# SwiGLU gate and up with the weights stationary: one product for all tokens, PSUM pools by stage, two banks by turns for the turned tokens

## The chip, the cores and the metric

The kernel runs on one core of one Trainium2 chip. The metric is device time in microseconds for one execution: the median of three runs, 1009.31 us, with 1009.22 as the lowest and 1009.62 as the highest. The profile is of one more execution of the same program.

The core has five engines with instruction queues of their own. TensorE (PE) multiplies matrices, VectorE (DVE), ScalarE (ACT) and GpSimd (POOL) work on vectors, and SyncE (SP) issues the DMA transfers. Each works through its own queue in order, and an instruction that needs another engine's result waits on a semaphore. PE writes to PSUM, which has eight banks of 512 fp32 columns; DVE and ACT read results from there.

## What is computed

Two layers, each a feed-forward block, a mixer and a second feed-forward block, for 256 tokens of width 1024 in fp32:

```python
def swiglu(x, w_in, w_out):
    gate, up = jnp.split(x @ w_in, 2, axis=-1)
    return (jax.nn.silu(gate) * up) @ w_out

for layer in range(DEPTH):                      # 2
    x = x + 0.5 * swiglu(rms_norm(x, norm_ffn1[layer]), w_ffn1_in[layer], w_ffn1_out[layer])
    h = rms_norm(x, norm_mix[layer])
    x = x + (conv_nsa_mixer(h, ...) if layer % 2 == 0 else stick_breaking_mixer(h, ...))
    x = x + 0.5 * swiglu(rms_norm(x, norm_ffn2[layer]), w_ffn2_in[layer], w_ffn2_out[layer])
return rms_norm(x, norm_final)
```

The inner width of a feed-forward block (FFN here) is 2816. The stages in time are FFN1, mixer 0, FFN2, FFN3, mixer 1, FFN4.

## The kernel before

**Precision.** PE multiplies in fp32r. Each operand is split into a high part and a low rest, and a product in fp32 quality is three products: high by high, high by low, low by high (`mm3`). A weight arrives by DMA in a tile `raw`; ACT copies it to `wh` in fp32r, DVE subtracts to get `wl` (`split`, lines 84 and 85). Both come in tiles of 128 x 1024. The activations get `XH` by an ACT copy that multiplies by the norm's gain (line 156) and `XL` by DVE (line 157).

**Turning.** Products need the width of x on the partitions. So x (128 tokens x 1024, two token tiles) is turned by PE's transposes, four 128 x 128 pieces into one PSUM bank (`turn_pe`, line 143), and each piece is evacuated by ACT (XH) and then by DVE (XL). The factor of the RMS norm is one number per token: ACT sums squares (line 126, `scr`), POOL adds (line 130, `ms`) and raises to -0.5 (line 131, `rs`). In front of a mixer x is multiplied by rs first (line 192, `xs`) and then turned. In front of an FFN x itself is turned and rs is applied later.

**FFN.** 11 chunks of 256 inner columns. For a chunk and a token tile, gate and up together are one PSUM bank of 512 columns (`gu`): the stationary operand is the 128 x 128 piece of XH or XL, the moving one 512 columns of weights. Eight pieces of the width by three products give 24 products of 512 columns per token tile and chunk, 528 in all (`gu_mm`). `act` applies rs with silu (line 226) and the product with up (line 228) per token. h then has tokens on the partitions and is turned for the second matrix (`act_turn`: PE's transposes, line 235, in pairs; ACT's `hh`, DVE's `hl`). The output products (`out_mm`, 264 of 512 columns) collect in four banks `po`; the last ones of each quarter are followed by the update of x (line 300).

**Order.** A scheduler sets the order of each engine's queue from the program; `flush` runs the turns that stand in `pending` at a place that the program names. At the start of an FFN that follows another stage the first chunk takes token tile 0 whole, calls `flush` after its fourth piece (so tile 1 is turned then), and goes on to tile 1. At the kernel's start loads, splits and evacuations of the first chunk are written in an order by hand. The three PSUM pools, `ps_gu` with 2 banks, `ps_tr` with 2 and `ps_po` with 4, are open throughout.

**Mixers.** Each begins with products of V (280 columns in mixer 0, 512 in mixer 1) and goes on to products of 256 columns (`project_T`, lines 353 to 355), each with a weight piece as the stationary operand. `OutProj` ends them, with the update of x in line 327.

Of the kernel before, what the change touches and what calls it, by code (L numbers as in the profile page):

```python
# [21 lines left out]
NCH = 11  # L22
# [24 lines left out]
def trunk_kernel(ctx: ExitStack, tc: tile.TileContext, a: dict):  # L47
# [13 lines left out]
    ps_gu = ctx.enter_context(tc.tile_pool(name="ps_gu", bufs=2, space=PSUM))  # L61
    ps_tr = ctx.enter_context(tc.tile_pool(name="ps_tr", bufs=2, space=PSUM))
    ps_po = ctx.enter_context(tc.tile_pool(name="ps_po", bufs=4, space=PSUM))

    def bank(pool, tag):
        return pool.tile([P, 512], F32, tag=tag, name=tag)

# [26 lines left out]
    nc.sync.dma_start(gains, a["gains"])  # L94
# [5 lines left out]
    gfin = [None]  # L100
    XH = [None]
    XL = [None]
    RS = [None]

    def new_xt():
        XH[0] = acts.tile([P, ND, T], F32R, tag="XH", name="XH")
        XL[0] = acts.tile([P, ND, T], F32R, tag="XL", name="XL")
# [3 lines left out]
    half = const.tile([P, 1], F32, name="half")  # L111
    G.memset(half, -0.5)
# [15 lines left out]
    def rms(t):  # L128
        ms = small.tile([P, 1], F32, tag="ms", name="ms")
        G.tensor_scalar(ms, sq[t][:, 0:1], sq[t][:, 1:2], EPS, op0=ALU.add, op1=ALU.add)  # L130
        latest["pool"] = G.tensor_tensor(RS[0][:, t:t + 1], ms, half, op=ALU.pow)
# [8 lines left out]
    def turn_pe(src):  # L140
        pt = bank(ps_tr, "tr")
        for k in range(4):
            PE.transpose(pt[:, k * P:(k + 1) * P], src[:, k * P:(k + 1) * P], ident)  # L143
        return pt

    def turn(t, hf, src, ni):

        pt = turn_pe(src)
        evacuate(pt, t, hf, ni, range(4))

    def evacuate(pt, t, hf, ni, ks):
        for k in ks:
            dt = hf * 4 + k
            g = gains[:, ni, dt:dt + 1]
            ts = slice(t * P, (t + 1) * P)
            latest["act"] = S.activation(XH[0][:, dt, ts], pt[:, k * P:(k + 1) * P], AF.Copy, scale=g)  # L156
            latest["dve"] = V.scalar_tensor_tensor(XL[0][:, dt, ts], pt[:, k * P:(k + 1) * P], g, f(XH[0][:, dt, ts]),  # L157
                                                   op0=ALU.mult, op1=ALU.subtract)
# [3 lines left out]
    def flush():  # L162
        for go in pending:
            go()
        pending.clear()

    def updated(t, hf, then):
# [5 lines left out]
        if kind == "ffn":  # L173
            pending.append(lambda: turn(t, hf, halves(t, hf), ni))
            if hf:
                rms(t)
            return
# [11 lines left out]
        if kind == "mix":  # L189
            for h in range(2):  # L190
                hs = slice(h * 512, (h + 1) * 512)
                V.tensor_scalar(o[:, hs], halves(t, h), r, None, op0=ALU.mult)
                pending.append(lambda h=h, hs=hs: turn(t, h, o[:, hs], ni))
# [18 lines left out]
    def ffn(w_in, w_out, then, first=None):  # L212
        xh, xl, rs = XH[0], XL[0], RS[0]
        po = {}
        hT = {}
# [6 lines left out]
        hs = {}  # L222

        def act(t, pg):
            sg = small.tile([P, T], F32, tag="sg", name="sg", bufs=2)
            latest["silu"] = S.activation(sg, pg[:, :T], AF.Silu, scale=rs[:, t:t + 1])  # L226
            h = small.tile([P, T], F32, tag="h", name="h", bufs=2)
            V.scalar_tensor_tensor(h, pg[:, T:], rs[:, t:t + 1], sg, op0=ALU.mult, op1=ALU.mult)  # L228
            hs[t] = h

        def act_turn(c, t):
            h = hs[t]
            pt = bank(ps_tr, "tr")
            for k in range(2):
                PE.transpose(pt[:, k * P:(k + 1) * P], h[:, k * P:(k + 1) * P], ident)  # L235
            hh = small.tile([P, 2, P], F32R, tag="hh", name="hh", bufs=6)
            hl = small.tile([P, 2, P], F32R, tag="hl", name="hl", bufs=6)
            pv = pt[:, :T].rearrange("p (k q) -> p k q", k=2)
            S.activation(hh, pv, AF.Copy)
            V.tensor_tensor(hl, pv, f(hh), op=ALU.subtract)  # L240
            hT[c, t] = hh, hl

        def out_mm(c, t, k, wo, hfs=(0, 1)):
            hh, hl = hT[c, t]
            wh, wl = wo[k]
            for hf in hfs:
# [3 lines left out]
                mm3(po[t, hf], hh[:, k], hl[:, k], wh[:, cs], wl[:, cs], c == 0 and k == 0, c == NCH - 1 and k == 1)  # L250

        wos = {}
        for c in range(NCH):
            if first and c == 0:
                w = first
            else:
                w = units(w_in[c, 0]) + units(w_in[c, 1])
            pg = [bank(ps_po, "po") if c == 1 else bank(ps_gu, "gu") for _ in range(NT)]
            if (c == 0 and not first) or c == NCH - 1:
                for t in range(NT):  # L260
                    for dt in range(ND):
                        gu_mm(pg[t], t, dt, w)
                        if c == 0 and t == 0 and dt == 3:
                            flush()
                        if c and t and dt == 2:
                            act_turn(c, 0)
                    act(t, pg[t])
# [703 lines left out]
```

## Time and profile before

| | |
|---|---|
| median of 3 runs | 1009.31 us (1009.22 to 1009.62) |
| the profiled execution | 1010.14 us |
| its span, first to last instruction | 1008.4 us |
| PE busy | 992.9 us, 98% |
| DVE busy | 598.7 us, 59% |
| ACT busy | 542.2 us, 54% |
| mean granted clock of PE | 0.999 of 2.4 GHz |

Times below are microseconds from the start of the span. Starts tell more than durations on PE: products are pipelined, one of 512 columns has a duration of 0.39 us, and the next starts 0.23 behind it. A bracket at the end of a timeline row is the idle time of the engine ahead of that row, and what ended it. In a row of the timeline equal instructions that follow each other are one row with their number behind an x.

### The profile page before, as it was taken

Reading aid. Unit: us, or ns where it says so; the run is one execution under the profiler, and the core shown is the slowest. Engines: PE = TensorE matmul, PEld = TensorE weight load, DVE = VectorE, ACT = ScalarE, POOL = GpSimd, SP = SyncE. Lnnn points to the kernel's source line nnn. Section 1 sums busy time; section 2 is a strip of 40 time slices with the busy share of each in tenths; the row PEclk is TensorE's granted clock in tenths of the full one; section 3 lists DMA queues with packets and bytes.
Section 4 is the critical chain, followed back from the end, with each engine's and each line's share of the span. In section 5 each row is a group of like instructions: output and inputs, shape, how many; then the busy total and the mean of one; then the engine's idle time right before and its main releaser. Section 6 shows DMA issues by size and latency. Waiting matters only on the chain.

```text
span 1008.4 us, 13048 instructions
## 1 busy us (share of the span) xinstructions
PE 992.9 (98%) x5048; PEld 825.3 (82%) x5048; DVE 598.7 (59%) x891; ACT 542.2 (54%) x944; POOL 51.5 (5%) x97
## 2 busy tenths in 40 slices
PE   8999999999999999999999999999999999999997
PEld 6888888788888888888878888887898788888885
DVE  5655555599855655555575555546777575555553
ACT  7544444587545544444474444445887474444443
POOL 4000000132111000000000000000000010000001
PEclk9999999999999999999999999999999999999999
DMA  8745454454433654545445454553632255554521
GB/s 319 271 170 205 170 206 135 146 194 161 164 126 110 228 205 169 206 170 204 168 168 201 175 200 175 198 177 125 247 118 98 84 205 210 172 204 172 204 105 42
DMA packets 26702, 176.72 MB, mean 175 GB/s; under 512 B 3344, under 2 KB 3472, under 8 KB 5904
## 3 DMA queue, kind: packets, MB, share of 16 engines
q1 hardware_dynamic: 26640, 175.89, 49.1%
q8 instruction: 39, 0.64, 0.3%
q14 instruction: 23, 0.19, 0.1%
HBM read 174.83 MB, written 1.05 MB: 174 GB/s over the span
## 4 chain that ended last, share of the span: by engine, by line
PE 74%; issue 18%; DVE 3%; ACT 2%; POOL 1%; DMA 1%; SPq 0%; POOLq 0%; ACTq 0%
PE gu L203 11%; PE gu L202 11%; PE gu L204 11%; PE po L202 8%; PE po L203 8%; PE po L204 8%; PE gu L353 3%; PE gu L355 3%; PE gu L354 3%; PE tr L235 1%; PE tr L143 1%; ACT wh L84 1%; DVE wl L85 1%; DMA raw<-in_w_in 1%; PE po L787 1%
## 5 line engine op out<-in xcount | busy, mean ns | idle before, releaser
L85 DVE TENSOR_TENSOR wl<-raw,wh 128x1024 fp32r<-128x1024 f32 (+3 forms) x388 | 397.2, 1038 | 295.1 <-ACT wh L84 293.8
L84 ACT ACTIVATE wh<-raw 128x1024 fp32r<-128x1024 f32 (+3 forms) x396 | 349.3, 899 | 317.0 <-PE gu L204 169.3
L202 PE MATMUL gu<-wh,XH 128*128 128x512 f32 (+1 forms) x688 | 267.6, 389 | 1.4 <-ACT XH L156 1.3
L204 PE MATMUL gu<-wh,XL 128*128 128x512 f32 (+1 forms) x688 | 266.9, 388 | 0.1
L203 PE MATMUL gu<-wl,XH 128*128 128x512 f32 (+1 forms) x688 | 266.6, 387 | 0.0
L202 PEld LDWEIGHTS gu<-wh,XH 128*128 128x128 f32 x688 | 129.1, 188 | 29.7 <-ACT XH L156 3.8
L204 PEld LDWEIGHTS gu<-wh,XL 128*128 128x128 f32 x688 | 129.1, 188 | 26.8 <-DVE XL L157 0.6
L203 PEld LDWEIGHTS gu<-wl,XH 128*128 128x128 f32 x688 | 129.2, 188 | 26.6 <-DVE wl L85 0.4
L202 PE MATMUL po<-wh,hh 128*128 128x512 f32 x352 | 143.9, 409 | 0.0
L204 PE MATMUL po<-wh,hl 128*128 128x512 f32 x352 | 138.0, 392 | 0.0
L203 PE MATMUL po<-wl,hh 128*128 128x512 f32 x352 | 137.8, 392 | 0.0
L353 PE MATMUL gu<-XH,wh 128*128 128x256 f32 x288 | 83.7, 291 | 1.6 <-DVE u L476 1.2
L355 PE MATMUL gu<-XH,wl 128*128 128x256 f32 x288 | 81.4, 283 | 0.0
L354 PE MATMUL gu<-XL,wh 128*128 128x256 f32 x288 | 81.4, 283 | 0.0
L204 PEld LDWEIGHTS po<-wh,hl 128*128 128x128 f32 x352 | 66.1, 188 | 14.1
L203 PEld LDWEIGHTS po<-wl,hh 128*128 128x128 f32 x352 | 66.4, 189 | 11.5
L202 PEld LDWEIGHTS po<-wh,hh 128*128 128x128 f32 x352 | 66.2, 188 | 11.3
L226 ACT ACTIVATE sg<-gu,rs 128x256 f32<-128x256 f32 x80 | 38.0, 475 | 61.3 <-PE gu L204 61.2
L353 PEld LDWEIGHTS gu<-XH,wh 128*128 128x128 f32 x288 | 55.1, 191 | 2.0 <-issue 1.3
L228 DVE SCALAR_TENSOR_TENSOR h<-gu,rs,sg 128x256 f32<-128x256 f32 x80 | 38.7, 483 | 30.2 <-ACT sg L226 30.2
L354 PEld LDWEIGHTS gu<-XL,wh 128*128 128x128 f32 x288 | 55.1, 191 | 0.1
L355 PEld LDWEIGHTS gu<-XH,wl 128*128 128x128 f32 x288 | 55.0, 191 | 0.0
(207 smaller groups left out, 874.5 us busy)
## 6 DMA issues: line engine op xcount, KB each, us to landing
raw<-in_w_in SPq DMA_DIRECT2D x86, 1024.0 KB, 4.7
raw<-in_w_out SPq DMA_DIRECT2D x44, 1024.0 KB, 4.7
raw<-in_w_ab SPq DMA_DIRECT2D x10, 1024.0 KB, 4.8
raw<-in_w_qk SPq DMA_DIRECT2D x8, 1024.0 KB, 4.8
raw<-in_w_out_ab SPq DMA_DIRECT2D x4, 1024.0 KB, 4.7
raw<-in_w_v SPq DMA_DIRECT2D x4, 1024.0 KB, 4.7
raw<-in_w_out_sb SPq DMA_DIRECT2D x4, 1024.0 KB, 4.9
raw<-in_w_in SPq DMA_DIRECT2D x8, 256.0 KB, 6.3
```

The costliest lines, as they stand in the source:

```text
L84: S.activation(h[:, ms], r[:, ms], AF.Copy)
L85: eng.tensor_tensor(l[:, ms], r[:, ms], f(h[:, ms]), op=ALU.subtract)
L143: PE.transpose(pt[:, k * P:(k + 1) * P], src[:, k * P:(k + 1) * P], ident)
L202: PE.matmul(out, lh, rh, start=first, stop=False)
L203: PE.matmul(out, lh, rl, start=False, stop=False)
L204: PE.matmul(out, ll, rh, start=False, stop=last)
L226: latest["silu"] = S.activation(sg, pg[:, :T], AF.Silu, scale=rs[:, t:t + 1])
L228: V.scalar_tensor_tensor(h, pg[:, T:], rs[:, t:t + 1], sg, op0=ALU.mult, op1=ALU.mult)
L235: PE.transpose(pt[:, k * P:(k + 1) * P], h[:, k * P:(k + 1) * P], ident)
L353: PE.matmul(pq, wh[:, dt], XH[0][:, dt], start=dt == 0, stop=False)
L354: PE.matmul(pq, wh[:, dt], XL[0][:, dt], start=False, stop=False)
L355: PE.matmul(pq, wl[:, dt], XH[0][:, dt], start=False, stop=dt == ND - 1)
```

## The change

Gate and up get their operands the other way round. The weights of w_in are laid out in 22 chunks of 128 inner columns. The stationary operand is a 128 x 128 piece of weights; the moving one is the tokens: `XX` holds XH and XL side by side, so wh meets all 512 columns of `XX` in one product (line 263), and wl meets the 256 columns of XH in another (line 265). The products stand in runs: for half of the width eight of 512 columns (four pieces, gate and up), then eight of 256. The result, in a pair of banks (gate and up; XL's half to be added to XH's half), has the inner columns on the partitions, so the transposes of h go away.

The factor rs now lies along the columns. `factor` spreads it over all partitions: ident times rs on DVE, one fp32 product with a matrix of ones on PE, a copy on ACT to `RB`. `act` then takes, per chunk: ACT copies the XL half out of PSUM, DVE adds the XH half, DVE multiplies by RB, ACT silu, DVE the product with up, ACT hh, DVE hl.

The PSUM pools other than `ps_po` are opened per stage (`stage`): in an FFN two pairs of banks, in a mixer two banks `gu` and two `tr`. They are closed at its end. `turn` puts pieces into two banks by turns; at the end of an FFN these two are the two halves of a gu pair (one tile), in a mixer two tiles `tr`, at the start of an FFN two banks of `po`. The first products of an FFN need all tokens. At the kernel's start both token tiles of a half are turned into the same banks and evacuated together, and the loads are reordered; chunk 0 and chunk 1 take their first halves, then their second ones. Between two FFNs the last output products go by halves of the width, (0,0), (1,0), (0,1), (1,1). The output products of chunk c-2 stand behind gu of chunk c.

The core of the diff:

```diff
-        def gu_mm(pg, t, dt, w):
-            (wh, wl), o = w[dt // 2], (dt % 2) * 512
-            ts = slice(t * P, (t + 1) * P)
-            mm3(pg, xh[:, dt, ts], xl[:, dt, ts], wh[:, o:o + 512], wl[:, o:o + 512], dt == 0, dt == ND - 1)
+        def gu_mm(c, w, i):
+            if c not in pgs:
+                pgs[c] = pair()
+            pg = pgs[c]
+            for wp in range(2):
+                for k in range(4):
+                    dt = 4 * i + k
+                    for s in range(2):
+                        lh = w[i][wp][:, (2 * k + s) * P:(2 * k + s + 1) * P]
+                        if wp == 0:
+                            PE.matmul(pg[:, s], lh, xx[:, dt].rearrange("p a q -> p (a q)"), start=dt == 0, stop=False)
+                        else:
+                            PE.matmul(pg[:, s, :T], lh, xx[:, dt, 0], start=False, stop=dt == ND - 1)
...
+        def factor():
+            dg = small.tile([P, 2, T], F32, tag="gus", name="dg", bufs=1)[:, 0]
+            for t in range(NT):
+                V.tensor_scalar(dg[:, t * P:(t + 1) * P], ident, rs[:, t:t + 1], None, op0=ALU.mult)
+            pr = bank(ps_po, "po")[:, :T]
+            PE.matmul(pr, ones, dg, start=True, stop=True)
+            S.activation(RB, pr, AF.Copy)
...
+                S.activation(gu[:, :, ts], pg[:, :, tl], AF.Copy)
+                V.tensor_tensor(gu[:, :, ts], pg[:, :, ts], gu[:, :, ts], op=ALU.add)
+                V.tensor_tensor(gu[:, :, ts], gu[:, :, ts], RB[:, None, ts].to_broadcast([P, 2, T // n]), op=ALU.mult)
+                latest["silu"] = S.activation(sg[:, ts], gu[:, 0, ts], AF.Silu)
+                V.tensor_tensor(sg[:, ts], gu[:, 1, ts], sg[:, ts], op=ALU.mult)
+                S.activation(hh[:, ts], sg[:, ts], AF.Copy)
+                V.tensor_tensor(hl[:, ts], sg[:, ts], f(hh[:, ts]), op=ALU.subtract)
...
+    def stage(mixer):
+        es = ExitStack()
+        for k in ("gu", "tr") if mixer else ("gu",):
+            st[k] = es.enter_context(tc.tile_pool(name="ps_" + k, bufs=2, space=PSUM))
+        return es
+    def pair(name="gu"):
+        return st["gu"].tile([P, 2, 512], F32, tag="gu", name=name)
...
+    def turn(t, dts, src, ni, get):
+        ts = slice(t * P, (t + 1) * P)
+        banks = get()
+        pt = {dt: banks[n % 2][:, n // 2 * P:(n // 2 + 1) * P] for n, dt in enumerate(dts)}
+        for dt in dts:
+            PE.transpose(pt[dt], src[:, dt * P:(dt + 1) * P], ident)
+        for dt in dts:
+            evacuate((XH[0][:, dt, ts], XL[0][:, dt, ts]), pt[dt], dt, ni)
...
+        order = [(0, 0), (1, 0), (0, 1), (1, 1)] if then[0] == "ffn" else [(0, 0), (0, 1), (1, 0), (1, 1)]
+        def banks():
+            both_ = pair()
+            return both_[:, 0], both_[:, 1]
```

The order of the built programs at three places. First PE at the kernel's start, behind the warm-up products. Line 143 before and line 932 now are transposes of x, lines 202 to 204 before and 263 and 265 now gate and up, line 244 the factor product. Before:

```order
L143 MATMUL tr<-ident,x 128x128 x8
L202 MATMUL gu<-wh,XH 128x512
L203 MATMUL gu<-wl,XH 128x512
L204 MATMUL gu<-wh,XL 128x512
...
L203 MATMUL gu<-wl,XH 128x512
L143 MATMUL tr<-ident,x 128x128 x8
L204 MATMUL gu<-wh,XL 128x512
```

Now:

```order
L932 MATMUL po<-ident,x 128x128 x16
L263 MATMUL gu<-XX,wh 128x512 x8
L265 MATMUL gu<-XX,wl 128x256 x8
...
L244 MATMUL po<-dg,ones 128x256
L263 MATMUL gu<-XX,wh 128x512 x8
```

Before, 20 products of gu stand between the two groups of eight transposes; now all sixteen stand ahead of the first, and the factor product stands behind four runs of sixteen.

Second DVE at the end of FFN1 and the entry into mixer 0. Lines 300 before and 338 now update x, 192 and 210 make xs, 157 and 162 evacuate a turned piece as the low part, 85 and 96 split weights. Before:

```order
L300 SCALAR_TENSOR_TENSOR x<-po,x 128x512
L157 SCALAR_TENSOR_TENSOR XL<-tr,gains,XH 128x128 x2
L85 TENSOR_TENSOR wl<-raw,wh 128x560
L157 SCALAR_TENSOR_TENSOR XL<-tr,gains,XH 128x128
L192 TENSOR_SCALAR xs<-x,rs 128x512 x2
L157 SCALAR_TENSOR_TENSOR XL<-tr,gains,XH 128x128 x8
```

Now:

```order
L338 SCALAR_TENSOR_TENSOR x<-po,x 128x512
L162 SCALAR_TENSOR_TENSOR XX<-gu,gains,XX 128x128
L210 TENSOR_SCALAR xs<-x,rs 128x512
L162 SCALAR_TENSOR_TENSOR XX<-gu,gains,XX 128x128
L210 TENSOR_SCALAR xs<-x,rs 128x512
L162 SCALAR_TENSOR_TENSOR XX<-gu,gains,XX 128x128 x4
L162 SCALAR_TENSOR_TENSOR XX<-tr,gains,XX 128x128 x8
```

Before, three pieces of tile 0 stand behind the last update of x, and their bank is not one that V's products write; now six pieces out of the gu pair stand there, one between the two xs and four behind them, and V's first product on PE waits for the last of them.

Third DVE where FFN3 follows FFN2, from the last update of x; line 242 makes dg. Before:

```order
L300 SCALAR_TENSOR_TENSOR x<-po,x 128x512
L85 TENSOR_TENSOR wl<-raw,wh 128x1024
L157 SCALAR_TENSOR_TENSOR XL<-tr,gains,XH 128x128 x2
L85 TENSOR_TENSOR wl<-raw,wh 128x1024
L157 SCALAR_TENSOR_TENSOR XL<-tr,gains,XH 128x128 x2
```

Now:

```order
L338 SCALAR_TENSOR_TENSOR x<-po,x 128x512
L96 TENSOR_TENSOR wl<-raw,wh 128x1024
L162 SCALAR_TENSOR_TENSOR XX<-gu,gains,XX 128x128
L242 TENSOR_SCALAR dg<-ident,rs 128x128
L96 TENSOR_TENSOR wl<-raw,wh 128x1024
L162 SCALAR_TENSOR_TENSOR XX<-gu,gains,XX 128x128
L162 SCALAR_TENSOR_TENSOR XX<-po,gains,XX 128x128 x2
L162 SCALAR_TENSOR_TENSOR XX<-gu,gains,XX 128x128
L162 SCALAR_TENSOR_TENSOR XX<-po,gains,XX 128x128 x2
L162 SCALAR_TENSOR_TENSOR XX<-gu,gains,XX 128x128
```

The splits stood among the evacuations before, too; but then the first gu products of tile 0 needed none of these. Now the first gu product waits for the last XX out of the gu pair in this list.

## Rows read from the trace of the kernel before

**Rows 1.** The page: busy time of each engine, share of the span, instructions.
```profile
PE 992.9 (98%) x5048; PEld 825.3 (82%) x5048; DVE 598.7 (59%) x891; ACT 542.2 (54%) x944; POOL 51.5 (5%) x97
```

**Rows 2.** Timeline of PE in FFN1 (start us, duration us, engine, line, operation).
```profile
65.49 0.39 PE L202 MATMUL po<-wh,hh 128*128 128x512 f32 x1
...
71.43 0.39 PE L202 MATMUL gu<-wh,XH 128*128 128x512 f32 x1
...
82.31 0.39 PE L202 MATMUL po<-wh,hh 128*128 128x512 f32 x1
```

**Rows 3.** Timeline of PE at the entry into the first mixer.
```profile
196.29 0.29 PE L202 MATMUL gu<-wh,XH 128*128 128x280 f32 x1
...
199.26 0.29 PE L204 MATMUL gu<-wh,XL 128*128 128x280 f32 x1
...
206.21 0.28 PE L353 MATMUL gu<-XH,wh 128*128 128x256 f32 x1
...
209.91 0.28 PE L354 MATMUL gu<-XL,wh 128*128 128x256 f32 x1
```

**Rows 4.** A window on FFN2: busy us of each engine, granted clock, DMA share, GB/s.
```profile
319.60:507.00 187.40, 187.40 (x853) 153.91 (x852) 106.41 (x130) 93.43 (x136) 2.56 (x4) 1.00 0.54 191
```

**Rows 5.** Timeline of PE at an fp32 product of 256 columns.
```profile
255.20 0.70 PE L675 MATMUL po<-pcT,VC 128*128 128x256 f32 x2
...
255.86 0.28 PE L354 MATMUL gu<-XL,wh 128*128 128x256 f32 x1
```

**Rows 6.** Group of one line (busy us, mean ns | idle before): copy of 512 from PSUM.
```profile
L794 ACT ACTIVATE e<-po 128x512 f32<-128x512 f32 x8 | 4.8, 599 | 2.0 <-PE po L789 1.9
```

**Rows 7.** Timeline of DVE where FFN3 follows FFN2.
```profile
508.26 0.68 DVE L300 SCALAR_TENSOR_TENSOR x<-po,x 128x512 f32<-128x512 f32 x1
508.86 1.22 DVE L85 TENSOR_TENSOR wl<-raw,wh 128x1024 fp32r<-128x1024 f32 x1
510.00 0.60 DVE L157 SCALAR_TENSOR_TENSOR XL<-tr,gains,XH 128x128 fp32r<-128x128 f32 x2
510.52 1.22 DVE L85 TENSOR_TENSOR wl<-raw,wh 128x1024 fp32r<-128x1024 f32 x1
```

**Rows 8.** The tile x in the first 14 us: how long its loads take to land.
```profile
DMA to landing us min/median/max: 3.4/5.5/6.8
```

**Rows 9.** Timeline of SyncE's DMA queue at the start: the last two loads of x.
```profile
4.06 0.91 SPq L859 DMA_DIRECT2D x<-in_x  x2
```

**Rows 10.** Timeline of PE at the start of the kernel.
```profile
1.24 4.02 PE L877 MATMUL gu<-warm 128*128 128x512 bf16 x9 [1.24 <-DVE warm L110]
...
9.69 0.76 PE L202 MATMUL gu<-wh,XH 128*128 128x512 f32 x2 [0.98 <-ACT XH L156]
...
13.84 0.48 PE L204 MATMUL gu<-wh,XL 128*128 128x512 f32 x1
```

**Rows 11.** Timeline of DVE at the entry into the first mixer.
```profile
196.57 0.68 DVE L300 SCALAR_TENSOR_TENSOR x<-po,x 128x512 f32<-128x512 f32 x1
...
199.24 1.82 DVE L192 TENSOR_SCALAR xs<-x,rs 128x512 f32<-128x512 f32 x2 [0.42 <-POOL rs L131]
...
202.20 0.61 DVE L157 SCALAR_TENSOR_TENSOR XL<-tr,gains,XH 128x128 fp32r<-128x128 f32 x2 [0.51 <-ACT XH L156]
202.99 0.61 DVE L157 SCALAR_TENSOR_TENSOR XL<-tr,gains,XH 128x128 fp32r<-128x128 f32 x2 [0.17 <-ACT XH L156]
```

**Rows 12.** Timeline of PE where FFN3 follows FFN2.
```profile
507.03 0.39 PE L202 MATMUL gu<-wh,XH 128*128 128x512 f32 x1
...
517.11 0.39 PE L202 MATMUL gu<-wh,XH 128*128 128x512 f32 x1
```

**Rows 13.** Timeline of PE at the entry into the second mixer.
```profile
695.85 0.39 PE L202 MATMUL gu<-wh,XH 128*128 128x512 f32 x1
...
718.99 0.28 PE L353 MATMUL gu<-XH,wh 128*128 128x256 f32 x1
```

**Rows 14.** Group of one line: the weight loads of the 256-column products.
```profile
L353 PEld LDWEIGHTS gu<-XH,wh 128*128 128x128 f32 x288 | 55.1, 191 | 2.0 <-issue 1.3
```

More of the change, by code (lines that the diff above doesn't have):

```diff
@@ L231, in act_turn @@
[L231 to L241, printed above, removed]
@@ new lines, in weights @@
+        def weights(c):
+            if first and c < 2:
+                return first[c]
+            return units(w_in[c])
+        def gu_mm(c, w, i):
[11 more added lines that the diff above has]
+                            PE.matmul(pg[:, s, :T], lh, xx[:, dt, 0], start=False, stop=dt == ND - 1)
@@ new lines, in out_mm @@
+                mm3(po[t, hf], hh[:, ts], hl[:, ts], wh[:, cs], wl[:, cs], c == 0, c == NF - 1)
+        es = stage(False)
+        w = [weights(0), weights(1)]
+        gu_mm(0, w[0], 0)
+        flush(lambda: two("po"))
+        gu_mm(1, w[1], 0)
+        gu_mm(0, w[0], 1)
+        factor()
+        act(0)
+        gu_mm(1, w[1], 1)
+        act(1)
+        for c in range(2, NF):
+            w = weights(c)
+            for i in range(2):
+                gu_mm(c, w, i)
+            act(c, NT if c == NF - 1 else 1)
+            if c % 2 == 0 and c < NF - 2:
+                wos[c // 2 - 1] = units(w_out[c // 2 - 1])
+            if c < NF - 2:
+                for t in range(NT):
+                    out_mm(c - 2, t)
@@ new lines, in ffn @@
+        if then == ("mix", 2):
+            switch("exp_and_others", latest["silu"])
+        for i in range(NF // 2 - 2, NF // 2):
+            wos[i] = units(w_out[i])
+        if then[0] != "end":
+            new_xt()
+        new_rs()
+        order = [(0, 0), (1, 0), (0, 1), (1, 1)] if then[0] == "ffn" else [(0, 0), (0, 1), (1, 0), (1, 1)]
+        def banks():
+            both_ = pair()
+            return both_[:, 0], both_[:, 1]
+        for t, hf in order[:2]:
+            for c in range(NF - 4, NF - 1):
+                out_mm(c, t, (hf,))
@@ L306, in trunk_kernel @@
+        for n, (t, hf) in enumerate(order):
+            for c in range(NF - 1 if n < 2 else NF - 4, NF):
+                out_mm(c, t, (hf,))
+                if c == NF - 3 and then[0] == "ffn":
+                    flush(banks)
+            V.scalar_tensor_tensor(halves(t, hf), po[t, hf], 0.5, halves(t, hf), op0=ALU.mult, op1=ALU.add)
+            if n == 2 and then[0] != "ffn":
+                flush(banks)
+            updated(t, hf, then)
+        es.close()
     class OutProj:
@@ L343, in rest @@
                     self.mm(1, n, (hf,))
+                    if hf and n == 4:
+                        flush(lambda: two("tr"))
                 if hf == 0:
-                    flush()
+                    flush(lambda: two("tr"))
                 self.done(1, hf)
@@ L751, in mixer1 @@
                     if dt == 4:
[L752 removed]
+                        flush(lambda: two("tr"))
                 S.activation(V1[:, t, hf * 512:(hf + 1) * 512], pv, AF.Copy)
[L754 to L755 removed]
+        _, YH, YL = parts("YY1")
         NQ = 2
```

228 lines of the change are left out of this document (87 added, 141 removed).

## The prediction

> **What bounds the kernel now.** I read the page first. TensorE (PE) is busy 992.9 of 1008.4 us [rows 1], so time changes only where PE does other work or stands. Then PE's timeline, for what a product costs: 48 products of 512 columns start within 10.88 us (71.43 to 82.31), 0.2267 each [rows 2]; 31 products of 256 columns, each with weights of its own, within 3.70 us, 0.120 each; 23 of 280 columns within 2.97, 0.129 each [rows 3]. From 65.49 to 71.43, 5.94 us, stand 24 output products and two pairs of transposes of h [rows 2]; 24 x 0.2267 is 5.44, so a pair costs 0.25. In FFN2 PE is busy in 187.40 of 187.40 us at a granted clock of 1.00 [rows 4]: what the vector engines do there is hidden. So the steady part can gain only by less work on PE, and the edges between stages, where PE now hardly stands, have much to lose. Those I read last.
>
> **The change, steady part.** Gate and up keep their columns: 528 products of 512 become 352 of 512 and 352 of 256. At the rates above that is 119.7 against 122.0 us per FFN, 2.3 more (every product carries a fixed piece, and there are 176 more). The 44 transposes, 22 pairs, go: 5.5 less. New is the factor product in fp32. An fp32 product of 256 columns runs before as two passes; it and one product behind it take 0.66 us [rows 5], so it costs 0.54. A run of eight 512s is followed by one of 256s, 44 times; that 512s and 256s of two kinds follow each other I price at 0 to 12 ns a change, the 13 ns being what a product takes beyond its columns (0.2267 against 512 columns at 2.4 GHz, 0.2133), so 0 to 0.5 us. Per FFN 5.5 - 2.3 - 0.54 - 0.25 = 2.4 less (2.1 to 2.7), **9.6 us less for four**.
> The new vector work does not reach PE there. For one chunk of 128 columns DVE has three weight splits of 1024 (1.14 each), the add and the multiplication (0.68 each, as the x update [rows 7]) and two shorter ones: at most 6.1 us, where PE needs 5.55 + 12 x 0.2267 = 8.27. ACT has less, its copy of 512 from PSUM at 0.60 [rows 6]. Two pairs of banks leave each pair a whole chunk's time to be read. I put nothing.
> The Trainium skill, "TensorE: Matmul & The Clock Gate", "Back-to-back issue gap", gives N/2.4 + 2.5 ns between starts, 109 and 216 ns here; by it 176 more products would cost 0.4 us a FFN in place of 2.3, the gain would be 17 us and the sum below 7 us lower. The rows show 120 and 227, and the measurement decides.
>
> **The change, edges.** With weights stationary one product takes all 256 tokens, so the first product of a FFN waits for XH and XL of both token tiles. Before, tile 0 began while tile 1 was still turned. And PSUM pools are closed by stage: the first product into the new pool waits for the last reader of the tile that lay there.
>
> (a) Start. All 16 transposes of x stand ahead of the first gu on PE. The last quarter of x is issued at about 4.54 us and landings took up to 6.8, so 11.3 [rows 8, 9]; the same 1.75 MB lie ahead of it after the change. With four transposes gu starts at 11.8, and with 20 products PE is at 16.3. Before, those 20 and all transposes are done at 13.84 [rows 10]. **+2.5.**
> (b) The first act. In FFN1 the factor product comes behind gu of chunk 1, and the third pair of banks is the first again: it waits for the copy of the factor (0.38 by a copy of 512 at 0.60 [rows 6] less half its columns), the copy of gus (0.60) and the add (0.68), with hops 1.9. In FFN2 to 4 half a chunk of products (2.8 us) stands between, which covers it. **+1.9.**
> (c) Into the first mixer. The turned xs of token tile 0 lies in a gu pair, both banks in one tile, and the first V product goes into its bank. So it waits for the eighth XX<-gu on DVE, and ahead of the last five of these DVE has the x update of the last half and both xs of tile 1. From the start of that update to that of xs 2.67 us pass, the two xs take 1.82 (POOL splits weights beside them), and XH and XL of one piece by turns 0.79 [rows 11]. The update begins 0.2 behind the last output product; one XL stands between the two xs, four pairs follow, the first with its ACT copy under xs: 0.2 + 2.67 + 0.26 + 1.82 + 0.35 + 3 x 0.79 = 7.7. I take 7.3, since XL overlaps its neighbours. Then 24 x 0.129 for tile 0, 0.87 for eight transposes, 0.5 until their first copy, 24 x 0.129 and 0.2 of small waits (two tr tiles let ACT and DVE work side by side): 15.1 us from the last output product to the first product of 256 columns. Before 9.92, from 196.29 to 206.21 [rows 3]. **+5.2.**
> (d) Into FFN2, and likewise FFN4. Behind the last output product DVE still has two splits of 1024, the x update and six XL before the first gu may go. The next start on DVE comes 1.14 behind a split, 0.60 behind an x update, 0.26 behind an XL [rows 7]: 2 x 1.14 + 0.60 + 5 x 0.26 + 0.35 + 0.24 for one ACT copy = 4.75; eight transposes (0.87) lie inside, so PE stands 3.9. Before, gu of tile 0 ran over it [rows 4], 0.2 was lost. **+3.7 each, +7.4.**
> (e) FFN2 into FFN3. gu waits for the last reader of the pair with x's turned tile. DVE: rest of a split 0.3, two XL 0.5, x update 0.6, a wait for ACT 0.2, two splits 2.28, XL and dg 0.4, an XL 0.35, then two pairs with ACT 1.58: 6.2, of which 0.87 transposes. Before, 37 products and 8 transposes (9.3) took 10.08 [rows 12], so 0.8 was lost. 5.3 - 0.8 = **+4.5.**
> (f) Into the second mixer, as (c), with splits of 1024 in the queue and no POOL beside: rest of a split 0.8, x update 0.6, XL and split 1.4, XL 0.35, two xs 0.9, XL 0.35, three pairs 2.4: 6.8. Before, 23.14 us [rows 13] held 96 products and eight transposes, 22.63, so 0.5 was lost. **+6.3.**
> The end (last output product to last store) keeps its order: 0.
>
> Sum: 2.5 + 1.9 + 5.2 + 7.4 + 4.5 + 6.3 = 27.8 against 9.6: +18.2. On the profiled execution 1010.14 + 18.2 = 1028.3; on the median, 0.8 lower, 1027.5.
>
> **The clock.** In (c) and (f) PE stands for about 7 us. No row shows such a pause: the longest behind the first product is 0.98, and the clock stayed. But at the start, having stood, PE took 4.02 us for nine products of 512 [rows 10], 0.447 each, the level of 1.2 GHz, before it went over to 2.4. A pause of 7 us is nearer to that one, so I let the clock fall in both; 4 us of work at half rate cost 2.0 each: +4.0. **Forecast 1031.5.** The Trainium skill (same page, "What's actually happening") has half rate as the default and activity as what releases it; the start row agrees, and no run here shows a pause of 4 to 7 us.
>
> **Rivals.**
> R1, the clock never falls: 1027.5. For it: 1.00 in FFN2 [rows 4]; against it nothing but the start.
> R2, it falls in the other pauses too: at the start (5 us without a product), in (e) (over 4 at a stretch), twice in (d) (3.9, with eight transposes between): four more times 2.0, 1039.5.
> R3, faster: the edges are covered as before, because the bank is given back before the pair's last reader, or ACT and DVE have done their splits earlier than their order says. (c) to (f) vanish, and 1009.3 - 9.6 + 4.4 = 1004 remain. It decides where less than 5 of the 23.4 us of (c) to (f) come true. Against it: DVE works its queue in order, and each wait above is for an instruction behind named others.
> R4, products of 256 in runs of eight do not keep 0.120, since each brings new weights. At 0.191, the time of a weight load [rows 14], 1408 of them cost 100 us more: 1131. Against it: the 31 products of before have the same form and a load each.
> R5, nothing to be measured: three quarters of (c) to (f) are covered by chance, and the rest eats the gain.
>
> **How the numbers follow.** Forecast 0.45, R1 0.22, R2 0.24, R3 0.05, R4 0.02, R5 0.02. Range: from R1 less 3.5 (the edges are sums of some 30 parts, good to 15%) to R2 and 2.5 more: 1024 to 1042; outside lie R3 to R5 and the tails of R1 and R2. A measurement of this kernel tells about 0.2% from no change. Faster 0.05, same 0.02, slower 0.93.
>
> **What would show it.** PE's timeline: gu starts near 11.8; 32 gu products in 5.55 us, no transposes inside; PE idle 7 us before the first product of each mixer, released by DVE's XX; about 4 in all before FFN2 and FFN4, over 4 before FFN3. Between their edges the FFNs are 2.4 us shorter. If the granted clock is below 1 at the mixers' entries, the clock term is right. If PE idles less than 3 us at (c) and (f), I am wrong there and the kernel may win.

## The result and the profile after

The changed kernel takes 1040.49 us in the median of four runs (1039.55 to 1044.43); the kernel before took 1009.46 beside it (four runs, 1009.22 to 1009.62). The ratio is 1.0315, with an interval of 1.0288 to 1.0342: slower by 3%. The forecast was 1031.5 with a range of 1024 to 1042. Sign and range held; the likeliest value was 9.0 us too low, and the time is that of rival R2.

The profiled execution took 1039.55, its span is 1037.8. The page, the lines that answer to [rows 1], and the granted clock by fortieths of the span:

```profile
PE 994.1 (96%) x5583; PEld 856.2 (83%) x5583; DVE 709.4 (68%) x1084; ACT 581.9 (56%) x1038; POOL 49.3 (5%) x94
...
PEclk9999999999999999999999999998999999999999
```

PE is busy 1.2 us longer than before, and the span is 29.4 longer: PE stands. (In its busy time the steady gain and the slower products of a low clock nearly cancel.) The vector engines have 111 us (DVE) and 40 us (ACT) more work. Where PE stands shows in its timeline. First the kernel's start [rows 10] and the first act:

```profile
9.69 1.97 PE L932 MATMUL po<-ident,x 128*128 128x128 f32 x8 [3.34 <-DMA x<-in_x]
11.31 2.81 PE L263 MATMUL gu<-XX,wh 128*128 128x512 f32 x8
...
23.29 0.60 PE L244 MATMUL po<-dg,ones 128*128 128x256 f32 x2
25.58 2.11 PE L263 MATMUL gu<-XX,wh 128*128 128x512 f32 x8 [1.69 <-DVE gus L278]
```

The first gu product starts at 11.31 (the forecast had 11.8), and behind the factor product PE waits for the add of gus. Next the steady part, one chunk of 128 columns in FFN2 [rows 2]:

```profile
424.13 1.98 PE L263 MATMUL gu<-XX,wh 128*128 128x512 f32 x8
425.94 1.12 PE L265 MATMUL gu<-XX,wl 128*128 128x256 f32 x8
...
432.44 1.75 PE L263 MATMUL gu<-XX,wh 128*128 128x512 f32 x7
```

Its 32 gu products and 12 output products take 8.31 us (424.13 to 432.44), without a transpose or a wait; the forecast's sum was 8.27. Then the entries into mixer 0 [rows 3], FFN2, FFN3 [rows 12], mixer 1 [rows 13] and FFN4:

```profile
198.76 0.39 PE L222 MATMUL po<-wh,hl 128*128 128x512 f32 x1
206.63 0.57 PE L220 MATMUL gu<-wh,XX 128*128 128x280 f32 x1 [7.49 <-DVE XX L162]
207.00 0.43 PE L221 MATMUL gu<-wl,XX 128*128 128x280 f32 x1
...
216.45 0.28 PE L394 MATMUL gu<-XX,wh 128*128 128x256 f32 x1
...
331.92 0.70 PE L170 MATMUL tr<-ident,x 128*128 128x128 f32 x4 [1.22 <-DVE XX L162]
332.77 0.66 PE L170 MATMUL po<-ident,x 128*128 128x128 f32 x4 [0.16 <-DVE x L366]
335.25 3.75 PE L263 MATMUL gu<-XX,wh 128*128 128x512 f32 x8 [1.83 <-DVE XX L162]
338.81 1.88 PE L265 MATMUL gu<-XX,wl 128*128 128x256 f32 x8
340.51 0.88 PE L263 MATMUL gu<-XX,wh 128*128 128x512 f32 x3
...
528.28 3.65 PE L263 MATMUL gu<-XX,wh 128*128 128x512 f32 x8 [4.09 <-DVE XX L162]
...
722.06 0.77 PE L220 MATMUL gu<-wh,XX 128*128 128x512 f32 x1 [7.04 <-DVE XX L162]
...
847.45 2.08 PE L263 MATMUL gu<-XX,wh 128*128 128x512 f32 x8 [1.83 <-DVE XX L162]
```

The brackets name XX on DVE at every entry. Behind four of the five the clock is low: eight products of 512 last 3.75 and 3.65 us at the start of FFN2 and FFN3, but 2.08 at the start of FFN4. Windows behind the five entries give the granted clock in the third column from the end:

```profile
206.00:212.00 6.00, 5.37 (x27) 5.40 (x28) 0.35 (x1) 0.10 (x1) 1.87 (x3) 0.60 0.48 169
...
336.00:341.00 5.00, 5.00 (x19) 4.24 (x18) 4.05 (x9) 2.22 (x4) 0.95 (x2) 0.55 0.57 210
...
528.00:533.00 5.00, 4.72 (x18) 4.00 (x19) 1.46 (x3) 1.04 (x1) 0.00 (x0) 0.66 0.63 218
...
722.00:727.00 5.00, 4.94 (x13) 3.98 (x14) 0.00 (x0) 0.00 (x0) 0.00 (x0) 0.58 0.01 3
...
847.00:852.00 5.00, 4.55 (x24) 3.94 (x25) 4.69 (x10) 3.42 (x8) 1.71 (x2) 1.00 0.65 226
```

Last DVE at the entry into mixer 0 [rows 11], and ACT beside it:

```profile
199.40 0.69 DVE L338 SCALAR_TENSOR_TENSOR x<-po,x 128x512 f32<-128x512 f32 x1
200.00 0.34 DVE L162 SCALAR_TENSOR_TENSOR XX<-gu,gains,XX 128x128 fp32r<-128x128 f32 x1
202.06 0.94 DVE L210 TENSOR_SCALAR xs<-x,rs 128x512 f32<-128x512 f32 x1 [1.73 <-POOL rs L148]
...
203.19 0.68 DVE L210 TENSOR_SCALAR xs<-x,rs 128x512 f32<-128x512 f32 x1
...
206.14 0.35 DVE L162 SCALAR_TENSOR_TENSOR XX<-gu,gains,XX 128x128 fp32r<-128x128 f32 x1 [0.44 <-ACT XX L161]
```

```profile
204.16 0.37 ACT L161 ACTIVATE XX<-gu,gains 128x128 fp32r<-128x128 f32 x1 [0.50 <-DVE XX L162]
204.95 0.37 ACT L161 ACTIVATE XX<-gu,gains 128x128 fp32r<-128x128 f32 x1 [0.42 <-DVE XX L162]
```

The x update, a wait of 1.73 for the factor, two xs and the last pieces out of the turned gu pair stand ahead of V's first product, as the order said. And the two engines wait for each other: ACT's read of a piece waits for DVE's read of the piece before, though the pieces lie in two banks, because both are one tile (with a tile for each bank they no longer do: e13_split_pair below).

### The profile page after: what moved, and what is told of

The parts are those of the page before. It is cut to its first block, busy times and chain, and to the rows that moved or that the text cites. A ratio compares the mean times of both kernels' runs of the same rounds, so it can differ in the third digit from the quotient of the medians.

```text
span 1037.8 us, 14410 instructions
## 1 busy us (share of the span) xinstructions
PE 994.1 (96%) x5583; PEld 856.2 (83%) x5583; DVE 709.4 (68%) x1084; ACT 581.9 (56%) x1038; POOL 49.3 (5%) x94
## 4 chain that ended last, share of the span: by engine, by line
PE 72%; issue 18%; DVE 4%; ACT 4%; POOL 1%; DMA 1%; SPq 0%; POOLq 0%; ACTq 0%; DVEq 0%
PE gu L263 24%; PE gu L265 12%; PE po L220 7%; PE po L221 7%; PE po L222 7%; PE gu L394 3%; PE gu L395 3%; PE gu L396 3%; ACT wh L95 1%; PE gu L220 1%; PE gu L222 1%; PE gu L221 1%; DVE wl L96 1%; ACT XX L161 1%; ACT scr L143 1%
## 5 line engine op out<-in xcount | busy, mean ns | idle before, releaser
L263 PE MATMUL gu<-XX,wh 128*128 128x512 f32 x1408 | 355.6, 395 | 9.4 <-DVE XX L162 7.8
L263 PEld LDWEIGHTS gu<-XX,wh 128*128 128x128 f32 x1408 | 260.7, 190 | 60.6 <-issue 8.4
L265 PEld LDWEIGHTS gu<-XX,wl 128*128 128x128 f32 x1408 | 193.1, 191 | 13.9
L265 PE MATMUL gu<-XX,wl 128*128 128x256 f32 x1408 | 197.1, 283 | 0.0
L280 ACT ACTIVATE sg<-gus 128x256 f32<-128x256 f32 (+1 forms) x92 | 37.4, 407 | 149.1 <-DVE gus L279 148.7
L394 PE MATMUL gu<-XX,wh 128*128 128x256 f32 x288 | 83.7, 291 | 1.6 <-DVE u L515 1.6
L396 PE MATMUL gu<-XX,wl 128*128 128x256 f32 x288 | 81.4, 283 | 0.0
L395 PE MATMUL gu<-XX,wh 128*128 128x256 f32 x288 | 81.4, 283 | 0.0
L279 DVE TENSOR_TENSOR gus<-gus,rb 128x512 f32<-128x512 f32 (+1 forms) x92 | 61.5, 669 | 3.0
L278 DVE TENSOR_TENSOR gus<-gu,gus 128x512 f32<-128x512 f32 (+1 forms) x92 | 60.9, 661 | 1.8 <-ACT gus L277 1.6
L281 DVE TENSOR_TENSOR sg<-gus,sg 128x256 f32<-128x256 f32 (+1 forms) x92 | 38.0, 413 | 34.0 <-ACT sg L280 33.8
L394 PEld LDWEIGHTS gu<-XX,wh 128*128 128x128 f32 x288 | 55.1, 191 | 2.2 <-issue 1.1
L277 ACT ACTIVATE gus<-gu 128x512 f32<-128x512 f32 (+1 forms) x92 | 53.3, 580 | 5.9 <-DVE gus L278 3.9
L395 PEld LDWEIGHTS gu<-XX,wh 128*128 128x128 f32 x288 | 55.1, 191 | 0.1
```

The lines of the kernel that those rows point to most:

```text
L263: PE.matmul(pg[:, s], lh, xx[:, dt].rearrange("p a q -> p (a q)"), start=dt == 0, stop=False)
L265: PE.matmul(pg[:, s, :T], lh, xx[:, dt, 0], start=False, stop=dt == ND - 1)
L278: V.tensor_tensor(gu[:, :, ts], pg[:, :, ts], gu[:, :, ts], op=ALU.add)
L279: V.tensor_tensor(gu[:, :, ts], gu[:, :, ts], RB[:, None, ts].to_broadcast([P, 2, T // n]), op=ALU.mult)
L394: PE.matmul(pq, wh[:, dt], XH[0][:, dt], start=dt == 0, stop=False)
L395: PE.matmul(pq, wh[:, dt], XL[0][:, dt], start=False, stop=False)
```

## The sum, step by step

Starts on PE of before and after, and what each stretch gave against the forecast (all of it with the clock at the forecast's 2.0 in (c) and (f)). The forecast's eight transposes ahead of FFN2 and FFN4 (0.87) count as a loss ahead of the first gu and as a gain behind it.

| up to | before | after | stretch gave | forecast | over |
|---|---|---|---|---|---|
| last output product of FFN1 | 196.06 | 198.76 | +2.70 | 2.5 + 1.9 - 2.4 = 2.0 | +0.7 |
| first 256 product, mixer 0 | 206.21 | 216.45 | +7.54 | 5.2 + 2.0 | +0.3 |
| last 256 product, mixer 0 | 295.08 | 305.81 | +0.49 | 0 | +0.5 |
| first gu of FFN2 | 319.61 | 335.25 | +4.91 | 3.7 + 0.87 | +0.3 |
| last output product of FFN3 | 695.63 | 714.63 | +3.36 | 4.5 - 4.8 - 0.87 = -1.17 | +4.5 |
| first 256 product, mixer 1 | 718.99 | 746.75 | +8.76 | 6.3 + 2.0 | +0.5 |
| first gu of FFN4 | 814.85 | 847.45 | +4.84 | 3.7 + 0.87 | +0.3 |
| last output product of FFN4 | 1001.10 | 1030.51 | -3.19 | -2.4 - 0.87 | +0.1 |

That is 29.4 measured and 22.2 forecast, 7.2 over; behind FFN4's last output product both executions have 9.04 left. 4.5 of the 7.2 lie in FFN2 and FFN3. There the clock was low behind both entries, which the forecast had not priced. The first run of eight 512s and eight 256s takes 2.77 us in the steady part (424.13 to 426.90). In FFN2 it takes 5.26 (335.25 to 340.51), since the 256s are slow there too, and in FFN3 4.44 (528.28 to 532.72): 2.5 and 1.7 lost, 4.2 together. What is left over is 0.4, so the steady gain came in FFN2 and FFN3, 2.4 and 2.2, as in FFN4 (2.3). FFN2, from its first gu product to its last output product, is 0.8 shorter than before; with the 2.5 of the clock, and without the 0.87 of the moved transposes, that is 2.4. In FFN1 the low clock took 0.8 at the start, where the eight products of 512 last 2.81 in place of 1.98.

## The experiments

The kernel of each run is the changed one with the edit shown, unless another is named. The medians of before beside them are 1009.5 to 1010.0 us.

### What is the clock's part: e3_busy

```diff
+        if then[0] == "mix":
+            idle = bank(ps_po, "po")
+            with tc.issue_after(latest["mm"].ins):
+                for i in range(33):
+                    PE.matmul(idle, warm[:, :P], warm, start=True, stop=True)
```

> The changed kernel with 33 bf16 products of 512 columns, the warm-up's kind, on PE between the last output product and the first V product of both mixers, into a po bank that nobody reads; they fill the pauses of 7.6 and 7.2 us. Theory (the low clock behind the pauses is from PE's standing): V's products of 280 columns start every 0.129 us again and not 0.233, those of 512 every 0.227 and not 0.427, which saves 2.5 and 1.9 us: 1036, and the waits themselves stay. Rival (the slow rate is from the readers of PSUM or of SBUF at that place): the spacings and the time stay, 1040.5.

Measured: 1037.14 us (1036.91 to 1037.41), ratio 1.027 [1.0252, 1.0287]. PE at the entry into mixer 0:

```profile
199.78 7.30 PE L346 MATMUL po<-warm 128*128 128x512 bf16 x33
207.44 0.37 PE L220 MATMUL gu<-wh,XX 128*128 128x280 f32 x1 [0.36 <-DVE XX L162]
207.64 0.29 PE L221 MATMUL gu<-wl,XX 128*128 128x280 f32 x1
207.77 0.29 PE L222 MATMUL gu<-wh,XX 128*128 128x280 f32 x1
```

V's first product still starts 8 us behind the last output product, but now V's products follow each other every 0.13 us in place of 0.23, and the granted clock is 1.00 in the windows at both mixers. Keeping PE at work without use gains 3.4 us: low clock at (c) and (f) costs about what the forecast gave it, 2.0 each (in the traces, 24 products of V take 5.05 in place of 3.18 us at (c), and 15 take 5.44 in place of 3.49 at (f)). The four runs lie within 0.5 us of each other, where those of the change lie within 4.9. The scatter of the change goes with the clock too: its runs have mean granted clocks of 0.985, 0.983, 0.981 and 0.977 and times of 1039.55, 1040.17, 1040.81 and 1044.43.

### Is the vector work hidden: e4_add_mult

```diff
+                if 1 < c < NF - 1:
+                    spare = small.tile([P, 2, T], BF16, tag="spare", name="spare", bufs=1)
+                    V.tensor_tensor(spare, gu, RB[:, None].to_broadcast([P, 2, T]), op=ALU.mult)
```

> The changed kernel with one more DVE instruction per chunk: gate and up times the factor are written a second time, to a tile that nobody reads, in chunks 2 to 20 of every FFN: 76 instructions, about 50 us more of DVE. Theory (vector work is hidden in the FFNs' steady part): within 1.5 us of 1040.5. Rival (the change lost its gain because DVE is too busy): 5 us or more on top.

Measured: 1043.49 us (1041.40 to 1044.79), 1.5 beyond what was expected. DVE is busy 755.0 us, 46 more. The period of a chunk on PE, and the window at the start of FFN4:

```profile
426.17 1.98 PE L263 MATMUL gu<-XX,wh 128*128 128x512 f32 x8
...
434.48 1.75 PE L263 MATMUL gu<-XX,wh 128*128 128x512 f32 x7
```

```profile
850.00:856.00 6.00, 6.00 (x21) 5.05 (x22) 5.10 (x9) 2.79 (x5) 1.52 (x2) 0.58 0.59 203
```

The period is 8.31 as without the added work, so in the steady part DVE's work costs nothing. In this execution the clock fell ahead of FFN4 too, and at a mean clock of 0.977 it took 1044.79 where the change took 1044.43 at the same clock. So the time over is the clock's. It fell ahead of FFN4 in the profiles of e1_tr_first, e3_busy and e5_early_add as well, without such work; whether more DVE work makes it fall more often, four runs do not tell.

### The first act: e5_early_add

```diff
-                V.tensor_tensor(gu[:, :, ts], pg[:, :, ts], gu[:, :, ts], op=ALU.add)
+                V.tensor_tensor(gu[:, :, ts], pg[:, :, ts], gu[:, :, ts], op=ALU.add)
+                if mid:
+                    mid()
...
-        factor()
-        act(0)
+        act(0, mid=factor)
```

(dg gets a tile of its own.)

> The changed kernel with the factor taken, in each FFN's first chunk, behind the copy and the add of gate and up and not ahead of them (dg in a tile of its own, since it shared gus's). Theory: the third pair of banks in FFN1 is given back as soon as gate and up are added, so PE's 1.95 us behind the factor product go: 1040.5 - 1.9 = 1038.6, with the scatter of the clock (1039.6 to 1044.4 without the edit) around it; in the profile the wait behind L244 is under 0.3 us. Rival (the wait only moves to the factor's own chain): 1040.5 and a pause of the same size elsewhere in FFN1.

Measured: 1040.56 us (1039.10 to 1041.22), no gain in the median. The wait itself is gone:

```profile
24.19 0.67 PE L244 MATMUL po<-dg,ones 128*128 128x256 f32 x2
24.51 0.47 PE L265 MATMUL gu<-XX,wl 128*128 128x256 f32 x1
24.81 2.00 PE L263 MATMUL gu<-XX,wh 128*128 128x512 f32 x8
```

PE goes on behind the factor product, and FFN1's last output product starts at 197.87 in place of 198.76. Behind the factor product 1.6 us are gained, so term (b) is right in its place; 0.8 of them had gone at the start, where gu began 0.22 later and the low clock cost its first eight products 0.57 more. The rest was lost in this execution ahead of FFN4, where the clock was 0.50 (845 to 850) in place of 1.00: the scatter of the clock is larger than this edit.

### Into FFN2 and FFN4: e6_po_turn

```diff
                     if hf and n == 4:
-                        flush(lambda: two("tr"))
+                        flush(lambda: two("po"))
```

> One line of the changed kernel: at the end of each mixer the turn of the second token tile's first half goes into two po banks, which are free, in place of the two tr banks that still hold the first tile's second half. Theory: before FFN2 and FFN4 the transposes no longer wait for a bank (1.38 us) and DVE gets these pieces earlier, so gu starts 2.5 to 3.5 us earlier at both; where the clock then stays up behind the shorter pause, 1.9 more: 1032 to 1036. Rival (the first gu waits for DVE's splits in the queue ahead, whatever the bank): 1040.

Measured: 1033.38 us (1032.77 to 1033.97), ratio 1.0233 [1.0218, 1.0248], as expected. Into FFN2:

```profile
331.09 0.40 PE L222 MATMUL po<-wh,YY 128*128 128x512 f32 x1
332.07 2.08 PE L263 MATMUL gu<-XX,wh 128*128 128x512 f32 x8 [0.58 <-DVE XX L162]
```

With the pieces of this place turned into two banks of po, no transpose waits any more for the pieces in tr to be read, and eight of them lie ahead of the last output products. 0.75 us of standing are left of 3.7 (0.75 is what lies between these two starts beyond a product's 0.23), and the clock stays up. Of the gain of 7.1 us some 6 are standing, 3 at each of two entries. The rest is the clock's: 2.5 saved at FFN2, less some 0.8 more at FFN3, where the first run of sixteen took 5.25 in place of 4.44 in this execution.

### The mixers' entries, by place: e1_tr_first

```diff
-        for k in ("gu", "tr") if mixer else ("gu",):
+        for k in ("tr", "gu") if mixer else ("gu",):
```

> The changed kernel with the mixers' two PSUM pools opened in the other order, so that V's first products and the turn of the second token tile trade places in the freed banks. Theory 1, the one of the prediction (a product waits for the last reader of the tile that lay in its bank): V's products now lie where an early read pair was, and start at once; PE's pauses of 7.6 and 7.2 us go or shrink below 3, and the time is some 10 us shorter, 1030. Theory 2 (a closed pool is given back as a whole, when the last of all its tiles is read): the pauses stay at 7.6 and 7.2 us and the time within the scatter, 1039 to 1045.

Measured, in one run: 1044.13 us at a mean clock of 0.977. PE's waits (us in total, times, longest):

```profile
PE gu L220 <- DVE XX L162: 14.5, 2, 7.5
```

That is the sum of the change's own waits, 7.49 and 7.04. In the built program of the change V's first products write bank 4, and the turned tile lies in banks 4 and 5, as the forecast had it. Here they write bank 6, of the other pair, which chunk 21 had left, and they wait as long. So it is not for its own bank that V's product waits; that a closed pool is given back as a whole (theory 2) fits.

### The pools and the pair: e8_open_pools and e13_split_pair

In the first, two pools of two single banks stay open throughout, and a pair is one bank of each:

```diff
-    st = {}
+    st = {k: ctx.enter_context(tc.tile_pool(name="ps_" + k, bufs=2, space=PSUM)) for k in ("gu", "tr")}
...
-        return st["gu"].tile([P, 2, 512], F32, tag="gu", name=name)
+        return [bank(st[k], k) for k in ("gu", "tr")]
...
-                S.activation(gu[:, :, ts], pg[:, :, tl], AF.Copy)
-                V.tensor_tensor(gu[:, :, ts], pg[:, :, ts], gu[:, :, ts], op=ALU.add)
+                for s in range(2):
+                    S.activation(gu[:, s, ts], pg[s][:, tl], AF.Copy)
+                    V.tensor_tensor(gu[:, s, ts], pg[s][:, ts], gu[:, s, ts], op=ALU.add)
```

> The changed kernel with its PSUM pools open throughout: a pair is two single tiles, gate from one pool of two banks and up from the other, and the mixers use the same pools, so nothing is closed and a product waits only for the readers of its own bank. Gate and up are therefore read out of PSUM by two instructions of 256 in place of one of 512 over both. Theory (the edges cost because the first product waits for the last reader of what lay there): PE's pauses before both mixers (7.6 and 7.2 us) and before FFN3 (4.3) go below 1.5 us, and with them the low clock behind each (2.5, 1.9 and 1.9 us): 1040.5 - 17 - 6 = about 1016, between 1010 and 1020. Rival A (the first products need the late pieces of XX anyway, so the pause only moves into them): above 1030. Rival B (the added work on DVE and ACT is what costs): no change or slower, 1040.

Measured: 1010.76 us (ten runs, 1010.35 to 1011.79), ratio 1.0009 [1.0000, 1.0019]: 29.7 less than the change, near the lower end of what was expected. Into mixer 0 (line numbers are three lower here):

```profile
199.57 0.39 PE L219 MATMUL po<-wh,hl 128*128 128x512 f32 x1
199.80 0.29 PE L217 MATMUL gu<-wh,XX 128*128 128x280 f32 x1
```

V starts 0.23 behind the last output product. But two things were changed. The second kernel keeps the split pair and closes the pools by stage again:

```diff
+        es = ExitStack()
+        for k in ("gu", "tr"):
+            st[k] = es.enter_context(tc.tile_pool(name="ps_" + k, bufs=2, space=PSUM))
+        return es
```

> The pools are opened and closed by stage, as in the change, but each pair is two tiles of one bank in two pools, and the two reads of a pair in act go bank by bank. It differs from e8_open_pools in one thing alone: there the same two pools stay open. Theory (a closed pool is given back as a whole, when its last reader is through): the pauses ahead of the mixers and ahead of FFN2 to FFN4 stay as with the change, 7 to 7.7 us ahead of each mixer, about 4 ahead of FFN3, and the time is about 1040. Rival (the tile of two banks is what couples V's first product to all eight turned pieces, and the pools have no part in it): the pauses ahead of the mixers fall below 1 us as in e8_open_pools, and the time is about 1011.

Measured, in one run: 1021.38 us at a clock of 0.993. Neither expectation holds; it lies between. DVE and PE into mixer 0, and PE into mixer 1:

```profile
198.76 0.34 DVE L162 SCALAR_TENSOR_TENSOR XX<-gu,gains,XX 128x128 fp32r<-128x128 f32 x1
199.02 0.34 DVE L162 SCALAR_TENSOR_TENSOR XX<-tr,gains,XX 128x128 fp32r<-128x128 f32 x1
...
201.17 0.35 DVE L162 SCALAR_TENSOR_TENSOR XX<-gu,gains,XX 128x128 fp32r<-128x128 f32 x1
201.44 0.34 DVE L162 SCALAR_TENSOR_TENSOR XX<-tr,gains,XX 128x128 fp32r<-128x128 f32 x1
201.95 1.84 DVE L210 TENSOR_SCALAR xs<-x,rs 128x512 f32<-128x512 f32 x2 [0.17 <-POOL rs L148]
```

```profile
201.66 0.37 PE L220 MATMUL gu<-wh,XX 128*128 128x280 f32 x1 [2.51 <-DVE XX L162]
```

```profile
705.40 0.47 PE L220 MATMUL gu<-wh,XX 128*128 128x512 f32 x1 [4.05 <-DVE XX L162]
...
706.01 0.63 PE L222 MATMUL gu<-wh,XX 128*128 128x512 f32 x1
706.44 0.63 PE L220 MATMUL gu<-wh,XX 128*128 128x512 f32 x1
```

With a tile for each bank the turned pieces are read in twos, and the last is through at 201.8, ahead of the xs; as one tile, ACT and DVE take turns over eight pieces, and the last four come behind both xs, to 206.5. So the pauses ahead of the mixers are two things. **One tile for two banks** makes one chain of its reads: with a tile for each, 7.65 and 7.20 us fall to 2.67 and 4.21, and (e) from 5.4 to 2.3. Behind the first the clock now stays at 1.00; into mixer 1 it still falls (products of 512 start 0.43 apart from 706.01 on, the granted clock of 706 to 709 is 0.50), and into FFN3 too (0.43 apart from 514.52 on). All this is worth some 19 us of the 30. The halved reads of act, which this kernel has besides, cost PE nothing in the steady part: a chunk takes 8.31 us here too. **Closing the pools** is worth the other 10 or 11, gone only where they stay open. In what way, this pair of runs does not show: with pools by stage V's first products write bank 4, which held four of the turned pieces, with open pools bank 5, so for what is left here the bank alone would do. That a closed pool holds back other banks as well rests on e1_tr_first alone. With one run of this kernel the two shares are good to a few us, no more.

### A faster version: e9_open_all, e10_open_start, e11_open_fill

The first is e8_open_pools with the edits of e5_early_add and e6_po_turn. The second also starts gu on the first half of the width and turns the second half of x behind that run of products; the third also fills the pause ahead of it with 16 products without use:

```diff
+                        with tc.issue_after(latest["gu"].ins) if hf else ExitStack():
+                            PE.transpose(pts[k % 2][:, (k // 2 * NT + t) * P:(k // 2 * NT + t + 1) * P],
...
+        half(0)
+        with tc.issue_after(latest["tp"].ins):
+            for i in range(16):
+                PE.matmul(idle, warm[:, :P], warm, start=True, stop=True)
+        return w, lambda: half(1)
```

> The kernel with open pools (1010.8 us), with the factor behind the first add (as in the run before) and the turn into po banks at the mixers' ends. Theory: the pieces add: 1.5 us at the first act, 1.4 + 0.3 + 0.5 at the entries of FFN2 and of FFN4 (the pauses of the open-pools run there), so 1010.8 - 1.5 - 4.4 = 1005, faster than the kernel before. Rival (another wait takes their place, DVE's queue at the entries above all): 1009 or more.

> As the run before, and at the kernel's start the transposes of x's second half stand behind the first run of sixteen gu products, not ahead of it. Theory of (a) (gu starts late since all 16 transposes stand ahead): gu starts at about 10 us and not 11.4, and PE is some 1 us further on behind the transposes: 1004. Rival (the weights' splits set the start, not the transposes): gu starts 1 us earlier, but waits for wl inside the run, and the time is that of the run before within 0.3 us.

> As the run before, with 16 more of the warm-up's bf16 products in PE's pause at the start, between the first eight transposes and the first gu product. Theory of the clock: the first gu products then start every 0.227 us and not 0.427 (in the open-pools run 14 products were at the slow rate, 2.5 us): 2 us less than the run before, 1002. Rival (they are slow for their weights, or the pause is too short to matter): no change, or later by what the 16 products overrun the pause.

Measured: 1004.55 (ratio 0.9943 [0.9931, 0.9956]), 1004.21 (0.9942 [0.9929, 0.9954]) and 1003.79 us (0.9939 [0.9925, 0.9952]). All three are faster than the kernel before, by 0.6%. The first came as expected; the other two can't be told from it, and the third lies 1.8 above what was expected. The last one's start:

```profile
9.37 0.58 PE L260 MATMUL gu<-XX,wh 128*128 128x512 f32 x1
...
21.36 0.28 PE L262 MATMUL gu<-XX,wl 128*128 128x256 f32 x1
23.45 0.67 PE L241 MATMUL po<-dg,ones 128*128 128x256 f32 x2 [1.81 <-DVE dg L239]
```

gu starts two us earlier than in e9_open_all (9.37 for 11.58) and at full clock, and the gain is given back at the factor product, which waits for dg and starts at 23.45; in e9_open_all it starts at 23.13, and in e10_open_start, which waits for dg as long, at 24.03: the norm's factor needs all of x, its squares on ACT and POOL's steps, and does not come earlier because gu does. Nor were the 2.5 us there that the expectation set on slow products: e8_open_pools has ten of them at the start (11.46 to 15.43), and they cost 1.9 us.

## Why the prediction was right, and where it was off

**The bound** was right: PE's stretches without a pause set the time, the work of DVE and ACT in the steady part is hidden (e4_add_mult), and the edges decide.

**The steady gain** of 2.4 per FFN was right: 2.2 to 2.4 came in FFN2 to FFN4. The products of 256 in runs kept the 0.120 [rows 3] (eight start within 0.96 us), so R4 is out.

**The edges** came within half a us of their terms: (a) gu at 11.31 for 11.8; (b) 1.95 for 1.9; (c) 7.65 for 7.3; (d) 3.7 for 3.9; (e) 5.4 for 5.3; (f) 7.20 for 6.8. What released PE was named rightly in each, but the reason was named wrongly in (c): V's bank was the turned tile's, as the forecast said, but moved away from it V waits as long (e1_tr_first), which fits a wait for the closed pool. And the wait is long for the eight pieces in one tile, whose pitch of 0.79 the forecast took from [rows 11] as given (e13_split_pair). That the number held in spite of the reason is luck: both lead to the same last XX.

**The clock** is the step that failed, a term of mis-sized extent. The forecast let it fall at (c) and (f) alone, 2 x 2.0. Each of these cost that: 3.4 us for both by e3_busy. But in the profiled execution it fell also ahead of FFN2 and FFN3, which cost 2.5 and 1.7, and the start lost 0.8. Ahead of FFN4, where it stayed up in that execution, it fell in the profiles of all four other kernels with this entry unchanged (e1_tr_first, e3_busy, e4_add_mult, e5_early_add). That was rival R2, at 0.24, with 2.0 for each of four pauses: in the profiles it is what happened, but for FFN4 in one of them. The choice went by length: (e) and (d) with their 4 us were put beside the 0.98 that had left the clock alone, not beside the 7. The rows of before could not tell between them, and a fall in some of these pauses would have been a better middle than a fall in none. The Trainium skill, "TensorE: Matmul & The Clock Gate", "What's actually happening", has the half rate as what is left when activity is missing. The rows agree in that, with 0.55 to 0.66 behind the pauses and 1.00 where products without use filled them.

**Small terms**: waits in mixer 0 cost 0.5 where nothing was put. Of the 9.0 us between forecast and median, 7.2 are in the table above; 0.8 is what the profiled execution of before lay above its median of then and 0.9 what that of after lay below its own.

**R3**, faster because the edges are covered, did not come; but its sum, 1004, is what the kernel takes once pools, tiles and turns are as in e9_open_all (1004.55). That the two agree so closely is chance: e9_open_all also takes term (b) away, which that sum keeps. The change's products were worth their gain all along; the tile over two banks and the pools by stage hid it.

## What to carry to other kernels

A PSUM tile over two banks is one thing to whoever orders the work: its readers on two engines take turns over all of it, and a pool closed between stages makes the next stage's first product wait for the last of them. Where an operand comes to need all tokens at once, price each stage's first product by the vector engine's queue ahead of its last input, and keep pools open and tiles of one bank where that product follows. Where PE stands for some microseconds, put down the low clock behind it as a cost of its own, with a chance, for every such pause.

## What was not expected of the hardware

The clock's fall is not settled by a pause's length alone. In the profiles of the changed kernel and its variants it was low behind each of the longest unfilled pauses: 7.49 and 7.04 us into the mixers, 4.09 into FFN3 with eight transposes ahead, 4.21 into mixer 1 of e13_split_pair. Behind shorter ones it went both ways: in e13_split_pair it fell at 2.3 us of standing into FFN3 and stayed at 1.00 behind 2.67 into mixer 0. Into FFN2 and FFN4, where PE stands 1.2, 0.2 and 1.8 us with four transposes between each, it fell in nine of ten cases (two entries in each of the change, e1_tr_first, e3_busy, e4_add_mult and e5_early_add): the first run of sixteen products takes 4.1 to 5.3 us there, and 2.87 at the tenth, FFN4 of the change. What decides it there stays open. The change's four runs differ by 4.9 us, and their times go with the clock; those of the kernel before beside them differ by 0.4 (of 24 later ones 23 lie within 1.6, and one took 1012.99 at a clock of 0.998).
